# One level of a Strassen-type algorithm in the feed-forward products of a two-block network

## The chip, the cores and the metric

The kernel runs on one core of a Trainium2 chip. The metric is the device time of one launch in microseconds (us); lower is better. Inputs and output lie in the chip's memory (DRAM), and everything is float32.

## The reference, cut to what matters

Block 1 (gated linear attention with a pooling branch) and the attention of block 2 are the same before and after. The change concerns the feed-forward part at the end of block 2 (`x` has 1024 tokens by 1024 features, `D_FF` is 2816):

```python
def causal_dwconv(u, w, b):          # three taps over the tokens
    up = jnp.pad(u, ((0, 0), (CONV_WIDTH - 1, 0), (0, 0)))
    out = b + w[0] * up[:, 0:s_len]
    for kk in range(1, CONV_WIDTH):
        out = out + w[kk] * up[:, kk:kk + s_len]
    return out
...
    x = x + o @ w_out[l]
    h = rmsnorm_2(x, ffn_norm_g[l])
    u = causal_dwconv(h @ w_up[l], conv_w[l], conv_b[l])     # [1024, 5632]
    gate, val = jnp.split(u, 2, axis=-1)
    x = x + (jax.nn.silu(gate) * val) @ w_down[l]            # [1024, 2816] @ [2816, 1024]
return rmsnorm_2(x, final_norm_g)
```

## The kernel before

Everything is kept with features on the 128 partitions and the 1024 tokens along a row. A tile of x is 128 features by 1024 tokens, and there are 8 of them (`x2`). A product of two float32 matrices is made of three matmuls, since each operand is split into a high and a low part of a reduced format (`mm3`, L235 to L238): low times high, high times low, high times high. The splitting of weights (`load`, L225) is a cast on ScalarE (ACT) and a subtraction on GpSimd (POOL, L182); that of activations is on ACT and VectorE (DVE), or on POOL. One matmul takes 128 x 128 weights and 512 columns, half a row of tokens, into one of 8 PSUM banks.

The output projection of block 2 ends the attention part. Its loop over 8 column tiles `ct` scales a PSUM bank by a norm, adds it to `x1` (that is `x2[ct]`), squares the sum on ACT, and adds the squares up in `acc`, on POOL and for the last tile on DVE. The same loop makes the parts `u3h` and `u3l` of x for the up projection, without the norm: `R3`, one over the root mean square of each token, is put on afterwards, where the bank of the up product is read (`p_`, in `conv`). So the first up tile can begin while `acc` isn't complete (`gemm_late` with `k0=6`, which puts the norm's sum between the parts).

The feed-forward part has 22 tiles `k` of the hidden width; each has a gate tile `k` and a value tile `22 + k`. `up_group` makes two of them: for each, 48 matmuls for the gate tile, 48 for the value tile, the convolution (ACT scales by one tap, DVE adds the two others), the sigmoid on ACT, two products on DVE, and the split into `fh` and `fl` (POOL). `down` then takes the two tiles and adds their products with `w_dn`, 96 matmuls, to the 8 tiles of `x2`, bank by bank, on DVE. The up products of the next group are put ahead of the down products of this one, so that TensorE always has work. The last group's down products, the final norm and the result go by parts of the tokens (`SEQ`).

The order of the work on each engine is that of the program after a scheduler has merged the streams. All DMAs of this part are issued by SyncE (SP), in order. PSUM banks and the slots of SBUF (pool `sb`, 32 slots of a row; `wpool` with 2 raw and 4 split weight buffers) come free when their last reader is done.

Of the kernel before, what the change touches and what calls it, by code (L numbers as in the profile page):

```python
# [17 lines left out]
P = 128  # L18
# [40 lines left out]
# columns of the vector table (one value per partition and column)  # L59
# [11 lines left out]
# columns of the constant table  # L71
# [7 lines left out]
# the first column tile of each block of w_mod  # L79
# [16 lines left out]
def fused_blocks(ctx, tc, io, out, dbg=None):  # L96
# [11 lines left out]
    wpool = ctx.enter_context(tc.tile_pool(name="wpool", bufs=1))  # L108
    sb = ctx.enter_context(tc.tile_pool(name="sb", bufs=1))
# [8 lines left out]

    def ld(name):
# [10 lines left out]
    def ht(name, dt=F32):  # L130
        return sb.tile([P, HALF], dt, tag="h", bufs=NH, name=f"{name}_{uid()}")
# [16 lines left out]
    # ---- constants  # L148
# [31 lines left out]
    # ---- arithmetic helpers  # L180
# [6 lines left out]
    def split(src, hi, lo, eng=None, scale=None):  # L187
        """src (times scale, one value per partition) = hi + lo exactly, both in float32r."""
# [7 lines left out]
    def defer(ins, on):  # L196
        """Keeps an early-ready load from being issued before another step of the program."""
# [6 lines left out]
    def log_exp_table(after):  # L204
        """Loads the table that has both functions, past the last use of another."""
# [3 lines left out]
    def rstd(total, r, n, scale=1.0 / D):  # L209
        """r = 1 / sqrt(total * scale + eps): exp(-ln / 2), then one Newton step."""  # L210
# [9 lines left out]
    def sigmoid(src, o):  # L220
        """o = 1 / (1 + exp(-src)) as exp(-ln(1 + exp(-src)))."""
# [4 lines left out]
    # ---- products: weights are split into two float32r parts as they come in  # L226
# [8 lines left out]
    def mm3(ps, ah, al, bh, bl, first, last):  # L235
        nc.tensor.matmul(ps, ah, bl, start=first, stop=False)  # L236
        nc.tensor.matmul(ps, al, bh, start=False, stop=False)  # L237
        nc.tensor.matmul(ps, ah, bh, start=False, stop=last)  # L238
# [3 lines left out]
    def gemm(parts, xh, xl, ranges=XH, c=P, c0=0, m=P, per=4, ks=range(KD), tag="pp"):  # L242
        """A tile of output columns; gives a bank of PSUM for each range of tokens."""
# [24 lines left out]
    def bank_rstd(acc, r, scale=1.0 / D, tag="pp"):  # L268
        """r = 1 / sqrt(mean + eps) from sums over all partitions of acc [128, 1024]."""
# [7 lines left out]
    def need(key):  # L277
        """Emits fillers up to the one called key."""
# [3 lines left out]
    def weave(fill, chain):  # L282
        """Emits each filler (key, step, function) before the given step of the chain."""
# [23 lines left out]
    x1_d = [dtile(f"x1_d{k}") for k in range(KD)]  # L307
    ra_d = dtile("ra_d")
# [7 lines left out]
    # ================================================================== block 1  # L316
# [3 lines left out]
    # conditioning vectors through silu  # L320
# [1030 lines left out]
```

## Time and profile before

| what | us |
| --- | --- |
| median of 3 runs | 2675.21 (2672.87 to 2677.45) |
| span of the profiled execution | 2679.3 |
| TensorE (PE) busy in it | 2549.1 (95%) |
| DVE, ACT, POOL busy | 1505.9 (56%), 961.0 (36%), 809.5 (30%) |

The profiled execution is one launch of its own; its span stands beside the median of the timed runs. Matmuls overlap in the records, since one begins before the last has drained: the distance from one start to the next is what a matmul costs, not its duration. Times of a waiting operation are longer than those of a free one where it waits for a shared resource after it has begun. The page's 40 slices show PE at 9 of 10 almost everywhere from the second slice on. The rows themselves stand in a section further down.

### The profile page before, as it was taken

How to read it: one execution, taken by the hardware profiler on the slowest of the kernel's cores; microseconds unless marked ns; L12 is line 12 of the kernel's file. 1: busy time of each engine (PE TensorE's matmuls, PEld its weight loads, DVE VectorE, ACT ScalarE, POOL GpSimd, SP SyncE). 2: the span in 40 equal slices, each digit the busy share in tenths (PEclk: the TensorE clock that was granted, in tenths of full speed). 3: DMA queues.
4: the chain of work that ended last, by engine and by line, in shares of the span. 5: the costliest groups of instructions: out<-in, count | busy, mean ns of one | idle time of the engine just before them, and what ended most of it. 6: DMA issues, size and time to landing. Idle time of an engine off the chain costs nothing. (4 is left out here: it accounts for less than half of the span.)

```text
span 2679.3 us, 36279 instructions
## 1 busy us (share of the span) xinstructions
PE 2549.1 (95%) x14390; PEld 2015.2 (75%) x14390; DVE 1505.9 (56%) x2190; ACT 961.0 (36%) x1634; POOL 809.5 (30%) x592
## 2 busy tenths in 40 slices
PE   6989999999999999999999999999899999999996
PEld 3878977777787888876777766666688888888885
DVE  6363292765927223255766677788934444444456
ACT  4342262553734412332333443433422222222233
POOL 1432221221212224434233222233433333333334
PEclk9989999999999999999999999999999999999998
DMA  6423242433424553335444323430111111111112
GB/s 256 125 74 108 86 158 85 151 111 101 145 80 146 196 193 110 118 103 155 127 127 127 113 77 114 124 105 28 40 49 49 48 48 48 47 48 48 48 48 75
DMA packets 109113, 270.55 MB, mean 101 GB/s; under 512 B 13600, under 2 KB 18592, under 8 KB 108944
## 3 DMA queue, kind: packets, MB, share of 16 engines
q1 hardware_dynamic: 101648, 244.90, 28.3%
q0 software_dynamic: 7296, 23.34, 3.7%
q8 instruction: 113, 1.85, 0.3%
q14 instruction: 56, 0.46, 0.1%
HBM read 192.40 MB, written 71.57 MB: 99 GB/s over the span
## 5 line engine op out<-in xcount | busy, mean ns | idle before, releaser
L182 POOL TENSOR_TENSOR wlo<-wraw,whi 128x512 fp32r<-128x512 f32 (+1 forms) x363 | 537.3, 1482 | 1639.2 <-ACT whi L190 1593.1
L190 ACT CAST whi<-wraw 128x512 fp32r<-128x512 f32 (+1 forms) x363 | 223.8, 617 | 709.4 <-PE pp L238 617.6
L236 PE MATMUL pp<-hl,whi 128*128 128x512 f32 (+1 forms) x768 | 312.1, 407 | 4.8 <-DVE hl L185 4.8
L237 PE MATMUL pp<-hh,wlo 128*128 128x512 f32 (+1 forms) x768 | 307.2, 400 | 0.4 <-POOL wlo L182 0.4
L238 PE MATMUL pp<-hh,whi 128*128 128x512 f32 (+1 forms) x768 | 306.4, 399 | 0.0
L238 PE MATMUL pp<-u3h,whi 128*128 128x512 f32 x688 | 271.4, 395 | 0.0
L237 PE MATMUL pp<-u3h,wlo 128*128 128x512 f32 x688 | 271.0, 394 | 0.0
L236 PE MATMUL pp<-u3l,whi 128*128 128x512 f32 x688 | 270.2, 393 | 0.0
L182 DVE TENSOR_TENSOR x<-x,pp 128x512 f32<-128x512 f32 (+1 forms) x184 | 121.5, 664 | 208.5 <-PE pp L238 208.5
L236 PEld LDWEIGHTS pp<-hl,whi 128*128 128x128 f32 (+1 forms) x768 | 144.9, 189 | 42.5 <-DVE hl L185 5.8
L237 PEld LDWEIGHTS pp<-hh,wlo 128*128 128x128 f32 (+1 forms) x768 | 144.8, 189 | 38.9 <-issue 6.1
L238 PEld LDWEIGHTS pp<-hh,whi 128*128 128x128 f32 (+1 forms) x768 | 144.9, 189 | 33.7 <-issue 0.4
L1028 DVE COPY pt<-pg 128x512 f32<-128x512 f32 (+2 forms) x192 | 101.0, 553 | 92.5 <-PE pg L1026 91.8
L237 PEld LDWEIGHTS pp<-u3h,wlo 128*128 128x128 f32 x688 | 129.0, 188 | 30.9
L236 PEld LDWEIGHTS pp<-u3l,whi 128*128 128x128 f32 x688 | 129.2, 188 | 30.3
L238 PEld LDWEIGHTS pp<-u3h,whi 128*128 128x128 f32 x688 | 129.1, 188 | 30.1
L236 PE MATMUL pp<-fl,whi 128*128 128x512 f32 (+1 forms) x368 | 142.0, 386 | 0.0
L238 PE MATMUL pp<-fh,whi 128*128 128x512 f32 (+1 forms) x368 | 141.4, 384 | 0.0
L237 PE MATMUL pp<-fh,wlo 128*128 128x512 f32 (+1 forms) x368 | 140.8, 383 | 0.0
L185 DVE SCALAR_TENSOR_TENSOR t<-p,vec,t 128x1023 f32<-128x1023 f32 x88 | 122.1, 1395 | 33.1 <-ACT t L1144 32.1
L237 PE MATMUL pp<-uh,wlo 128*128 128x512 f32 x336 | 139.2, 414 | 0.0
L236 PE MATMUL pp<-ul,whi 128*128 128x512 f32 x336 | 138.3, 412 | 0.0
(384 smaller groups left out, 5434.0 us busy)
## 6 DMA issues: line engine op xcount, KB each, us to landing
wraw<-in_w_up SPq DMA_DIRECT2D x88, 256.0 KB
wraw<-in_w_qk SPq DMA_DIRECT2D x48, 256.0 KB
wm<-in_w_mod SPq DMA_DIRECT2D x24, 512.0 KB
wraw<-in_w_dn SPq DMA_DIRECT2D x44, 256.0 KB
x<-in_xT SPq DMA_DIRECT2D x16, 512.0 KB
wraw<-in_w_v SPq DMA_DIRECT2D x32, 256.0 KB
wraw<-in_w_out SPq DMA_DIRECT2D x32, 256.0 KB
q<-qs_d POOLq DMA_DIRECT2D x16, 512.0 KB, 5.0
```

The source lines that it names most:

```text
L182: return (eng or nc.vector).tensor_tensor(out=o, in0=a, in1=b, op=op)
L185: return (eng or nc.vector).scalar_tensor_tensor(out=o, in0=a, scalar=s, in1=b, op0=op0, op1=op1)
L190: nc.scalar.copy(hi, src)
L236: nc.tensor.matmul(ps, ah, bl, start=first, stop=False)
L237: nc.tensor.matmul(ps, al, bh, start=False, stop=False)
L238: nc.tensor.matmul(ps, ah, bh, start=False, stop=last)
L1028: nc.vector.tensor_copy(o, ps[:, :w])
```

## The change

Write the up product of one pair (gate tile `k` and value tile `22 + k`) as a 2 x 2 block product: the two tiles by two halves of the 1024 input features, times the two halves of the features by two halves of the tokens. Such a product needs 8 block products of 12 matmuls (4 tiles of 128 features, 3 matmuls each), or 7 with sums of blocks as operands (`seven` gives the weight side, `T` the x side). The change makes 7, in the order 1, 6, 2, 5, 7, 3, 4. Banks `al`, `be` and `ga` are added to by two or three products each, and read out in between. The down product is made the same way in four groups of 3, 3, 2 and 2 pairs of tiles (`DN_GROUPS`; tiles 20 and 21 are left to plain products at the end, as before). There each product's 4 banks take 12 matmuls from every pair of the group.

The operands must be split after they are summed, so the norm is put on x first (`normed`), and 28 parts of x are made ahead of the loop, every other lower part on POOL. All weights are summed by DVE as they come and split by ACT and POOL. The buffers don't hold both stages: x2 is written to DRAM (`x2_d`) and read again for the down stage, and each gated tile is written to `f_d` and read again. The pools are closed and opened anew at the start of the up products and of the down products; a pool `keep` of 8 rows stays (and the main pool of the earlier parts has 24 slots and not 32).

```diff
-NSLOT, NF, NT, NLD, NH, NQT = 32, 3, 2, 3, 5, 5
+NSLOT, NKEEP, NF, NT, NLD, NQT = 24, 8, 3, 2, 3, 5
+UP_RAW, UP_SUM, UP_W, UP_E = 6, 4, 5, 5
+DN_RAW, DN_SUM, DN_W = 34, 14, 3
+DN_GROUPS = [[(0, 3), (1, 4), (2, 5)], [(6, 9), (7, 10), (8, 11)], [(12, 14), (13, 15)], [(16, 18), (17, 19)]]
...
+        nc.sync.dma_start(x2_d[ct], x1)
...
-        u3h.append(b1k("u3h", F32R))
-        u3l.append(b1k("u3l", F32R))
-        split(x2[ct], u3h[ct], u3l[ct], None, V("ffg", ct))
-    R3 = b1k("R3")
-    u0, = gemm_late(
-        [[load(io["w_up"][0, j], 4, P) for j in range(2)]], u3h, u3l, tags=["lg"], k0=6, then=lambda: bank_rstd(acc, R3, tag="pg"),
-    )
...
+    for a, b in XH:
+        ps = get("pg")
+        nc.tensor.matmul(ps, ones, acc[:, a:b], start=True, stop=True)
+        total.append(ps)
+    front.close()
...
+    for ps in total:
+        R3.append(seg("R3", "R3", 2))
+        rstd(ps, R3[-1], HALF)
...
+    def xparts(src):
+        turn[0] += 1
+        return parts(src, "t", 28, nc.gpsimd if turn[0] % 2 else None)
...
+    for j in range(4):
+        T[1].append(xparts(normed(j, LOW)))
+    for j in range(4):
+        T[2].append(xparts(normed(j + 4, LOW)))
+    for j in range(4):
+        b12, b22 = normed(j, HIGH), normed(j + 4, HIGH)
+        b11, b21 = x2[j][:, LOW], x2[j + 4][:, LOW]
+        t3, t2 = seg("t3", "e", UP_E), seg("t2", "e", UP_E)
+        tt(t3, b22, b12, ALU.subtract)
+        tt(t2, t3, b11, ALU.add)
+        T[6].append(xparts(t2))
+        T[7].append(xparts(t3))
+        tt(b21, b21, t2, ALU.subtract)
+        tt(b12, b12, b11, ALU.subtract)
...
+    def seven(a11, a12, a21, a22, s1, s2):
+        yield 1, a11
+        tt(s1, a21, a22, ALU.add)
+        tt(s2, s1, a11, ALU.subtract)
+        yield 6, s2
+        yield 2, a12
+        yield 5, s1
+        tt(a11, a11, a21, ALU.subtract)
+        yield 7, a11
+        tt(s2, a12, s2, ALU.subtract)
+        yield 3, s2
+        yield 4, a22
...
+        for n, src in seven(*raw, s1, s2):
+            w = parts(src, "w", UP_W, nc.gpsimd)
+            wh, wl = (x.rearrange("p (k c) -> p k c", k=4) for x in w)
+            bank = {1: al, 2: al, 7: ga, 4: ga}.get(n, be)
+            for j in range(4):
+                th, tl = T[n][j]
+                mm3(bank, wh[:, j], wl[:, j], th, tl, j == 0 and n in (1, 6, 7), j == 3, True)
+            if n == 1:
+                p1 = seg("p1", "e", UP_E)
+                nc.scalar.copy(p1, al)
+            elif n == 2:
+                nc.scalar.copy(pg[:, LOW], al)
+            elif n == 6:
+                u = seg("u", "e", UP_E)
+                tt(u, p1, be, ALU.add)
...
+        tt(tg, tg, pg, ALU.mult)
+        tt(tg, tg, tv, ALU.mult)
+        nc.sync.dma_start(f_d[k], tg)
+    back.close()
...
+            for j in range(len(pairs)):
+                m, src = next(As[j])
+                wh, wl = parts(src, "w", DN_W, nc.gpsimd)
+                th, tl = parts(tsum(n, B[j], S[j]), "t", DN_W, nc.gpsimd if j else None)
+                for c in range(4):
+                    cs = slice(c * P, c * P + P)
+                    mm3(banks[c], wh[:, cs], wl[:, cs], th, tl, j == 0 and n in (1, 6, 7), j == len(pairs) - 1, True)
...
+                o = x2[o[0]][:, o[1]]
+                tt(o, o, banks[c], ALU.add)
+            if n == 1 and g == len(DN_GROUPS) - 1:
+                for c in range(4):
+                    for ct, half in ((c, HIGH), (c + 4, LOW), (c + 4, HIGH)):
+                        o = x2[ct][:, half]
+                        tt(o, o, p1[c], ALU.add, nc.gpsimd)
```

First place: POOL at the start of the up products. Before, after the last addition of squares (`acc`), it splits weights of the up products (`wlo`) and then the first gated tile (`fl`):

```order
L182 TENSOR_TENSOR wlo_16737<-wraw_16735,whi_16736 128x512
L182 TENSOR_TENSOR wlo_16743<-wraw_16741,whi_16742 128x512
L182 TENSOR_TENSOR wlo_16806<-wraw_16804,whi_16805 128x512
L182 TENSOR_TENSOR wlo_16812<-wraw_16810,whi_16811 128x512
L182 TENSOR_TENSOR fl_16730<-t_16646,fh_16729 128x1024
L182 TENSOR_TENSOR wlo_16883<-wraw_16881,whi_16882 128x512
L182 TENSOR_TENSOR wlo_16889<-wraw_16887,whi_16888 128x512
```

After, `lo` of `x_` and `t_` are operands of x (14 of them, the last ten shown), `lo_16770` ahead of these belongs to the weights of the first product, `lo_16790` to those of the second:

```order
L195 TENSOR_TENSOR lo_16649<-t_3061_16645,hi_16648 128x512
L195 TENSOR_TENSOR lo_16665<-t_3067_16661,hi_16664 128x512
L195 TENSOR_TENSOR lo_16681<-t_3073_16677,hi_16680 128x512
L195 TENSOR_TENSOR lo_16697<-t_3079_16693,hi_16696 128x512
L195 TENSOR_TENSOR lo_16707<-x_2764_15301,hi_16706 128x512
L195 TENSOR_TENSOR lo_16715<-x_2829_15573,hi_16714 128x512
L195 TENSOR_TENSOR lo_16723<-x_2886_15836,hi_16722 128x512
L195 TENSOR_TENSOR lo_16731<-x_2943_16099,hi_16730 128x512
L195 TENSOR_TENSOR lo_16739<-x_2886_15836,hi_16738 128x512
L195 TENSOR_TENSOR lo_16747<-x_2943_16099,hi_16746 128x512
L195 TENSOR_TENSOR lo_16790<-s_3113_16763,hi_16789 128x512
L195 TENSOR_TENSOR lo_16808<-wr_16756,hi_16807 128x512
```

The weights of the first pair's second product moved behind all the operands of x.

Second place: DVE in the middle of the up products. Before, the read-out of two banks (`p`), then the convolution's two steps (L185), the product with the sigmoid and that of gate and value:

```order
L182 TENSOR_TENSOR p_16879<-pp_16893,R_3051_16562 128x512
L182 TENSOR_TENSOR p_16879<-pp_16919,R_3051_16562 128x512
L185 SCALAR_TENSOR_TENSOR t_16880<-p_16879,vec,t_16880 128x1023
L185 SCALAR_TENSOR_TENSOR t_16880<-p_16879,vec,t_16880 128x1022
L182 TENSOR_TENSOR p_16948<-pp_16962,R_3051_16562 128x512
L182 TENSOR_TENSOR t_16880<-t_16880,sgf_17017 128x1024
L182 TENSOR_TENSOR p_16948<-pp_16988,R_3051_16562 128x512
L185 SCALAR_TENSOR_TENSOR t_16949<-p_16948,vec,t_16949 128x1023
L185 SCALAR_TENSOR_TENSOR t_16949<-p_16948,vec,t_16949 128x1022
L182 TENSOR_TENSOR t_16880<-t_16880,t_16949 128x1024
```

After, from the read-out of one pair's last but one bank to the `u` of the next (`s_` are sums of weights, L198 the convolution's steps, `pv` and `pg` the tiles that the banks go to):

```order
L195 TENSOR_TENSOR pg_17682<-p_3301_17703,pp_17685 128x512
L195 TENSOR_TENSOR s_3352_17986<-wr_17982,wr_17984 128x512
L195 TENSOR_TENSOR s_3353_17987<-s_3352_17986,wr_17978 128x512
L198 SCALAR_TENSOR_TENSOR t_17813<-pg_17682,vec,t_17813 128x1023
L195 TENSOR_TENSOR pv_17683<-u_17723,pp_17686 128x512
L198 SCALAR_TENSOR_TENSOR t_17813<-pg_17682,vec,t_17813 128x1022
L198 SCALAR_TENSOR_TENSOR t_17817<-pv_17683,vec,t_17817 128x1023
L195 TENSOR_TENSOR t_17813<-t_17813,pg_17682 128x1024
L198 SCALAR_TENSOR_TENSOR t_17817<-pv_17683,vec,t_17817 128x1022
L195 TENSOR_TENSOR u_17876<-p_3331_17856,pp_17838 128x512
```

The read-out `pv` of product 4 and that of the next pair's product 6 (`u`) now have convolution steps and a product ahead of them. On ACT the copy of the next pair's first bank (`p_`, L1240) stands behind the sigmoid (L1268) there:

```order
L1260 ACTIVATE t_17660<-pg_17529,vec 128x1024
L203 CAST hi_17761<-wr_17672 128x512
L1260 ACTIVATE t_17664<-pv_17530,vec 128x1024
L1268 ACTIVATE pg_17529<-t_17660 128x1024
L1240 COPY p_3301_17703<-pp_17684 128x512
L203 CAST hi_17779<-s_3293_17681 128x512
```

Third place: SP where the up products end. Before, the loads of weights go on in a row, of the up tiles and of the down tiles:

```order
L231 DMA wraw_21098<-in_w_up 128x512
L231 DMA wraw_21168<-in_w_dn 128x512
L231 DMA wraw_21206<-in_w_dn 128x512
L231 DMA wraw_21244<-in_w_dn 128x512
L231 DMA wraw_21282<-in_w_dn 128x512
L231 DMA wraw_21320<-in_w_dn 128x512
```

After, with `q_` the blocks of the first down group, from `f_d` and from the weights:

```order
L1273 DMA f_d_206<-t_19802 128x1024
L1273 DMA f_d_207<-t_19955 128x1024
L1291 DMA q_20129<-f_d_187 128x512
L1291 DMA q_20131<-f_d_190 128x512
L1291 DMA q_20133<-f_d_187 128x512
L1291 DMA q_20135<-f_d_190 128x512
L1291 DMA q_20137<-in_w_dn 128x512
L1291 DMA q_20139<-in_w_dn 128x512
L1291 DMA q_20141<-in_w_dn 128x512
L1291 DMA q_20143<-in_w_dn 128x512
L1291 DMA q_20145<-f_d_188 128x512
L1273 DMA f_d_208<-t_20108 128x1024
```

Loads of the first down group are issued ahead of the write of the last gated tile (`f_d_208`), and the rest of them, 15 loads and then the 8 of x2, behind it.

## Rows read from the trace of the kernel before

**Rows 1.** Page, part 1: busy time, share of the span, instructions, by engine.
```profile
PE 2549.1 (95%) x14390; PEld 2015.2 (75%) x14390; DVE 1505.9 (56%) x2190; ACT 961.0 (36%) x1634; POOL 809.5 (30%) x592
```

**Rows 2.** Windows: start:end, length, busy us (x instructions) by engine, granted clock, DMA.
```profile
1900.00:1950.00 50.00, 37.92 (x146) 28.51 (x145) 41.79 (x40) 20.52 (x24) 23.12 (x12) 0.90 0.12 37
...
2000.00:2050.00 50.00, 50.00 (x217) 40.55 (x217) 26.32 (x30) 11.72 (x14) 13.64 (x9) 1.00 0.16 48
...
2350.00:2400.00 50.00, 50.00 (x218) 40.50 (x217) 28.77 (x32) 14.63 (x17) 17.30 (x11) 1.00 0.17 48
...
2550.00:2600.00 50.00, 50.00 (x217) 40.52 (x216) 29.19 (x32) 14.63 (x17) 17.28 (x12) 1.00 0.16 47
```

**Rows 3.** Time line of TensorE, 1905 to 1931: start, us, operation, [idle before <-releaser].
```profile
1905.55 0.47 PE L236 MATMUL lg<-u3l,whi 128*128 128x512 f32 x1 [3.71 <-DVE t L182]
...
1907.04 0.63 PE L236 MATMUL lg<-u3l,whi 128*128 128x512 f32 x1
...
1907.46 0.63 PE L237 MATMUL lg<-u3h,wlo 128*128 128x512 f32 x1
...
1924.35 3.52 PE L272 MATMUL pg<-acc,ones 128*128 128x512 f32 x4 [7.67 <-DVE acc L182]
...
1930.47 0.39 PE L236 MATMUL pp<-u3l,whi 128*128 128x512 f32 x1
```

**Rows 4.** Time line of DVE, 1882 to 1931.
```profile
1882.08 1.28 DVE L182 TENSOR_TENSOR x<-x,t 128x512 f32<-128x512 f32 x2
...
1883.99 0.69 DVE L182 TENSOR_TENSOR x<-x,t 128x512 f32<-128x512 f32 x1
...
1886.73 2.90 DVE L182 TENSOR_TENSOR x<-x,t 128x512 f32<-128x512 f32 x1
...
1889.55 2.31 DVE L185 SCALAR_TENSOR_TENSOR u3l<-x,vec,u3h 128x1024 fp32r<-128x1024 f32 x1
...
1911.54 1.27 DVE L182 TENSOR_TENSOR t<-lg,rs 128x512 f32<-128x512 f32 x2
...
1930.57 0.68 DVE L185 SCALAR_TENSOR_TENSOR R<-rt,R 128x512 f32<-128x512 f32 x1
```

**Rows 5.** Time line of POOL, at the change-over and at 2039.
```profile
1886.52 2.56 POOL L182 TENSOR_TENSOR acc<-acc,sq 128x1024 f32<-128x1024 f32 x1 [4.40 <-ACT sq L1122]
...
1889.03 1.74 POOL L182 TENSOR_TENSOR wlo<-wraw,whi 128x512 fp32r<-128x512 f32 x1
...
1910.68 3.21 POOL L182 TENSOR_TENSOR acc<-acc,sq 128x1024 f32<-128x1024 f32 x1
...
2039.86 1.30 POOL L182 TENSOR_TENSOR wlo<-wraw,whi 128x512 fp32r<-128x512 f32 x1 [6.15 <-ACT whi L190]
```

**Rows 6.** Groups by line and form, 1940 to 2600: count, busy us, mean ns, idle before.
```profile
L182 POOL TENSOR_TENSOR wlo<-wraw,whi 128x512 fp32r<-128x512 f32 x120 | 164.0, 1367 | 392.8 <-ACT whi L190 392.6
...
L182 POOL TENSOR_TENSOR fl<-t,fh 128x1024 fp32r<-128x1024 f32 x21 | 51.1, 2433 | 60.8 <-ACT fh L190 60.8
...
L182 DVE TENSOR_TENSOR x<-x,pp 128x512 f32<-128x512 f32 x144 | 99.0, 688 | 194.9 <-PE pp L238 194.9
...
L185 DVE SCALAR_TENSOR_TENSOR t<-p,vec,t 128x1023 f32<-128x1023 f32 x41 | 58.6, 1429 | 30.8 <-ACT t L1144 30.8
...
L182 DVE TENSOR_TENSOR t<-t,sgf 128x1024 f32<-128x1024 f32 x21 | 25.7, 1225 | 4.4 <-ACT sgf L1166 4.1
...
L1166 ACT ACTIVATE sgf<-t 128x1024 f32<-128x1024 f32 x21 | 22.3, 1062 | 56.3 <-DVE t L185 56.3
```

**Rows 7.** Time lines of SP and ACT at the start: a load's issue, loads landing.
```profile
0.76 0.39 SPq L150 DMA_DIRECT2D vec<-in_vec  x1
...
2.95 0.21 ACT L322 ACTIVATE tsi<-vec 128x16 f32<-128x16 f32 x1 [0.92 <-DMA vec<-in_vec]
...
13.20 1.06 ACT L340 ACTIVATE sq<-x 128x1024 f32<-128x1024 f32 x1 [0.29 <-DMA x<-in_xT]
...
14.48 1.06 ACT L340 ACTIVATE sq<-x 128x1024 f32<-128x1024 f32 x1 [0.22 <-DMA x<-in_xT]
```

More of the change, by code (lines that the diff above doesn't have):

```diff
@@ L117, in b1k, with xk @@
         return bt(name, dt)[:, :L]
+    def xk(name, dt=F32):
+        return keep.tile([P, SLOT], dt, tag="x", bufs=NKEEP, name=f"{name}_{uid()}")[:, :L]
     def ld(name):
@@ L233, in load, with mm3 @@
         return hi.rearrange("p (k c) -> p k c", k=kh), lo_.rearrange("p (k c) -> p k c", k=kh)
[L235 to L238, printed above, removed]
+    def mm3(ps, ah, al, bh, bl, first, last, again=False):
+        nc.tensor.matmul(ps, ah, bl, start=first, stop=False, skip_group_check=again)
+        nc.tensor.matmul(ps, al, bh, start=False, stop=False, skip_group_check=again)
+        nc.tensor.matmul(ps, ah, bh, start=False, stop=last, skip_group_check=again)
     XH = [(0, HALF), (HALF, L)]
@@ L307, in fused_blocks @@
     x1_d = [dtile(f"x1_d{k}") for k in range(KD)]
+    x2_d = [dtile(f"x2_d{k}") for k in range(KD)]
+    f_d = [dtile(f"f_d{k}") for k in range(NFF)]
     ra_d = dtile("ra_d")
@@ L1110, in fused_blocks @@
     )
-    u3h, u3l = [], []
     acc = b1k("acc3")
@@ L1139, in conv @@
-    def conv(ct, banks=None):
-        p_, t = b1k("p"), b1k("t")
-        for ps, a, b in banks or gemm([load(io["w_up"][ct, j], 4, P) for j in range(2)], u3h, u3l):
-            tt(p_[:, a:b], ps, R3[:, a:b], ALU.mult)
+    total = []
+    for a, b in XH:
[3 more added lines that the diff above has]
+    front.close()
+    back = ExitStack()
+    sb = back.enter_context(tc.tile_pool(name="up", bufs=1, reuse_waits="tile"))
@@ new lines, in fused_blocks, with seg, parts @@
+    tags["h"] = ("e", UP_E)
+    def seg(name, tag, bufs, dt=F32):
+        return sb.tile([P, HALF], dt, tag=tag, bufs=bufs, name=f"{name}_{uid()}")
+    def parts(src, tag, bufs, eng):
+        hi, lo_ = seg("hi", tag + "h", bufs, F32R), seg("lo", tag + "l", bufs, F32R)
+        split(src, hi, lo_, eng)
+        return hi, lo_
+    R3 = []
+    for ps in total:
+        R3.append(seg("R3", "R3", 2))
+        rstd(ps, R3[-1], HALF)
+    es.close()
+    es = ExitStack()
+    get = psum_pool(es, pp=(HALF, 8))
@@ new lines, in fused_blocks, with normed @@
+    LOW, HIGH = slice(0, HALF), slice(HALF, L)
+    turn = [0]
+    def xparts(src):
+        turn[0] += 1
+        return parts(src, "t", 28, nc.gpsimd if turn[0] % 2 else None)
+    def normed(k, half):
+        x = x2[k][:, half]
+        stt(x, x, V("ffg", k), R3[0 if half is LOW else 1], ALU.mult, ALU.mult)
+        return x
+    T = {n: [] for n in range(1, 8)}
+    for j in range(4):
+        T[1].append(xparts(normed(j, LOW)))
+    for j in range(4):
+        T[2].append(xparts(normed(j + 4, LOW)))
@@ new lines, in fused_blocks @@
+    for j in range(4):
[9 more added lines that the diff above has]
+    for j in range(4):
+        T[5].append(xparts(x2[j][:, HIGH]))
+    for j in range(4):
+        T[3].append(xparts(x2[j + 4][:, HIGH]))
@@ L1144, in conv @@
+    def conv(ct, p_):
+        t = xk("t")
         nc.scalar.activation(t, p_, AF.Identity, scale=V("cw", 88 + ct), bias=V("cb", ct))
@@ L1176, in down @@
-    def down(grp, wd, c2, fh, fl, ranges=XH):
-        for cc in range(2):
-            ct = 2 * c2 + cc
-            for ps, a, b in gemm([wd], fh, fl, ranges, c0=cc * P, per=2, ks=range(2)):
-                tt(x2[ct][:, a:b], x2[ct][:, a:b], ps, ALU.add)
-    def load_down(grp, c2):
-        return load(io["w_dn"][grp, c2], 2, DV)
-    f = up_group(0)
-    for grp in range(NFF // 2 - 1):
-        nf = up_group(grp + 1)
-        for c2 in range(4):
-            down(grp, load_down(grp, c2), c2, *f)
-        f = nf
@@ L1193, in fused_blocks @@
-    wd = [load_down(NFF // 2 - 1, c2) for c2 in range(4)]
-    rF = b1k("rF")
+    for k in range(NFF):
+        pg, pv = up_pair(k)
+        tg, tv = conv(k, pg), conv(NFF + k, pv)
+        i = nc.scalar.activation(pg, tg, AF.Sigmoid)
+        if k == NFF - 1:
+            log_exp_table(i)
+        tt(tg, tg, pg, ALU.mult)
+        tt(tg, tg, tv, ALU.mult)
+        nc.sync.dma_start(f_d[k], tg)
+    back.close()
+    sb = ctx.enter_context(tc.tile_pool(name="down", bufs=1, reuse_waits="tile"))
@@ new lines, in fused_blocks, with in_half @@
+    fl_, wl_ = {}, {}
+    for k in (NFF - 2, NFF - 1):
+        for h, half in enumerate((LOW, HIGH)):
+            f = raw_tile("f")
+            nc.sync.dma_start(f, f_d[k][:, half])
+            fl_[k, h] = parts(f, f"f{k}{h}", 1, None)
+            w = raw_tile("wl")
+            nc.sync.dma_start(w, io["w_dn"][k, h])
+            wl_[k, h] = parts(w, f"v{k}{h}", 1, nc.gpsimd)
+    rF = [raw_tile("rF") for _ in range(2)]
+    def in_half(a, b):
+        return a // HALF, slice(a % HALF, a % HALF + b - a)
@@ L1196, in final, with last_down @@
+    def last_down(a, b):
+        h, ts = in_half(a, b)
+        for ct in range(KD):
+            cs = slice(ct % 4 * P, ct % 4 * P + P)
+            ps = get("pp")[:, : b - a]
+            for k in (NFF - 2, NFF - 1):
+                (wh, wl), (th, tl) = wl_[k, ct // 4], fl_[k, h]
+                mm3(ps, wh[:, cs], wl[:, cs], th[:, ts], tl[:, ts], k == NFF - 2, k == NFF - 1)
+            tt(x2[ct][:, a:b], x2[ct][:, a:b], ps, ALU.add)
     def final(a, b):
-        g = L // (b - a)
+        g = HALF // (b - a)
+        h, ts = in_half(a, b)
@@ L1226, in fused_blocks @@
         a, b = RNG[n]
+        h, ts = in_half(a, b)
         if what == "product":
-            for c2 in range(4):
-                down(NFF // 2 - 1, wd[c2], c2, *f, [(a, b)])
+            last_down(a, b)
         elif what == "squares":
```

146 lines of the change are left out of this document (102 added, 44 removed).

## The prediction

> **What bounds the kernel now.** I read the page's busy shares first, then the windows of the last 800 us, then the time lines around 1900 us. TensorE is busy 95% of the span [rows 1]. In the feed-forward part it is never idle: 50 us hold 217 or 218 matmuls, the granted clock is 1.00 (2.4 GHz), while DVE, ACT and POOL are busy 11 to 29 of 50 us and the DMA engines a sixth of the time [rows 2]. A 512-column matmul therefore costs 50/217.5 = 0.230 us, and each one that disappears there is worth 0.230 us as long as the others keep up. The one hole is the change-over from the output projection: the window from 1900 has 146 matmuls, 72 fewer (16.5 us). There TensorE waits for DVE's last addition of squares until 1924.35 and has finished the 48 matmuls of the first up tile at 1930.47 [rows 3].
>
> **What is removed.** Up: 22 x 2 tiles x 48 = 2112 matmuls become 22 x 7 products x 12 = 1848. Down: 20 of 22 tiles of the gated product, 960 matmuls, become 10 pairs x 7 x 12 = 840; the last two stay. That is 384 fewer, 384 x 0.230 = **88.4 us** less if TensorE stays as full as it was.
>
> **What two engines do to each other.** The price of everything added depends on one pattern of the change-over. A DVE addition of two SBUF tiles of 512 takes 0.69 us alone, 0.60 from one to the next (1882.08 and 1883.99 [rows 4]). At 1886.73 it takes 2.90 us: POOL has been in a 1024-wide addition since 1886.52 and ends at 1889.08 [rows 5]. POOL's next subtraction (1889.03) takes 1.74 us against 1.30 alone (2039.86 [rows 5]), and DVE's 1024-wide step at 1889.55 takes 2.31, against 1.2 for one of its size (1225 ns [rows 6]). So each waits until the other has nearly ended: POOL shuts DVE out for about 1.14 us with 512 elements and 2.28 with 1024, DVE shuts POOL out for about 0.60 and 1.20. A DVE operation that reads PSUM isn't touched: two at 1911.54 take 1.27 us in the midst of a POOL addition that runs from 1910.68 to 1913.89. The Trainium skill has this as a rule (GPSIMD Engine Reference, 1. Specifications): POOL's SBUF interfaces are shared with VectorE and contend with its operations that have two SBUF inputs. The rows of this trace agree; without the contention the sum would be that of the first rival.
>
> Before, in the feed-forward part, this costs nothing: POOL has 141 subtractions in 660 us [rows 6], some 7 per k of 33 us (144 matmuls). The change adds weight sums and operand sums on DVE, two SBUF inputs each, and raises POOL's subtractions to 7 in 19.3 us (84 x 0.230).
>
> **1. Start of the up products.** No product can begin before the norm R3 now, since x2 is normed first. The parts that DVE made for the old up products (u3l) go, which helps: DVE needs per column tile 4 x 0.60 plus one POOL addition of 2.28, 4.7 us; x of tile 1 is done at 1884.7 [rows 4], six tiles later it is 1912.9, and with the square and the last addition the sum of squares is there at about 1914 instead of 1924.35. From there to the low half of the norm 6.9 us pass, as before (1924.35 to 1931.25 [rows 3, 4]): 1920.9. Then DVE has 41 operations on SBUF pairs until the last of the operands t2 (norms, sums, every other lower part), 41 x 0.60 = 24.6, with 7 POOL subtractions between, 7 x 1.14 = 8.0. POOL's queue has all 14 lower parts of the operands ahead of the weights of the second product (the first of the orders above): 8 more subtractions against a busy DVE, 8 x 1.74 = 13.9. The second product starts at 1967.4, and about 2 us go to the clock, which after a hole of 3.71 us fell so that eight matmuls were 0.43 apart instead of 0.23 (1905.55 and 1907.04 [rows 3]). By then 12 matmuls are done; before, 48 were done at 1930.47. Loss: (1969.4 - 1930.5) + 36 x 0.230 = **47 us**. If the engines didn't shut each other out, DVE's 53 operations take 31.8 us, and the loss is 30; with a hop lost at some of the casts, 55.
>
> **2. The 22 pairs.** Per pair the shared side carries POOL 7 x 1.14 = 8.0 and DVE 4 weight sums x 0.60 and 6 operations of 1024 (4 convolution steps, 2 products) x 1.20 = 9.6, together 17.6 of 19.3 us: it fits, with little room. But a PSUM bank is now taken up again two products later, so TensorE waits for DVE and ACT inside a pair (the second order). From the end of product 4 of one pair to the start of product 5 of the next TensorE has 3 products, 8.3 us; in that time DVE's queue has the eviction pv (0.60), three convolution steps (3 x 1.20), one product with the sigmoid (1.20) and then the eviction u that product 5 waits for (0.69): 6.1 us alone [rows 6], 9.5 with three POOL subtractions between. ACT's copy p1, for which product 2 waits, stands behind the sigmoid, and that behind a convolution step. I take 1.0 us a pair, **22 us**; from 0 (DVE's 6.1 us fit) to 40 (DVE's 9.6 and five evictions of 0.69, and POOL's 8.0, all one after the other: 21.1 us a pair).
>
> **3. From up to down.** Before, the two stages were interleaved and there was no seam. Now the down loads take buffers of the closed pool, and SP has the write of the last gated tile in the midst of them (the third order). That write waits for the convolution of the last pair: after the last matmul an eviction, two steps, sigmoid, two products, some 7 us from [rows 6], 9 with POOL between. Behind it 12 loads of 256 KB must land until the third weight quarter of product 1 is there. 512 KB land every 1.28 us [rows 7], so the write and the 12 loads take 1.3 + 7.7 us at least, plus some 2.2 us from issue to landing (vec, 0.76 to 2.95 [rows 7]) and 1.3 + 0.6 for cast and subtraction. TensorE goes on 21 us after its last up matmul, and has done two products of 2.76 us in between: 15.5, with 2 us for the clock **18 us**; 12 if the write comes at 6 us, 28 if loads run at half that rate for a while.
>
> **4. Down.** A group of three pairs has 252 matmuls, 58.0 us. POOL: 21 weight and 14 operand parts, 35 x 1.31 = 45.9 us alone; DVE: 24 sums and 7 parts, 31 x 0.60 = 18.6. If each DVE operation delays POOL, POOL needs 64.5 us: 6.5 lost in each of two groups. A group of two has 38.6 us of TensorE; POOL 27.5 (32.7 in the third group, which also splits the last weights) and DVE 13.8: 2.7 and 8 lost. In the last group 12 additions of p1 to x2 stand in POOL's queue between two products (15.7 us), and TensorE has one product of 5.5 us and three buffers to cover them: some 10 of it are seen. All of it is 13 + 8 + 2.7 + 10 = 34, with half the delays 22: I take **27 us**, from 11 (the 12 additions alone) to 40 (and a late evicted bank in each product group).
>
> **5. At nothing.** The x2 writes (8) and gated-tile writes (22) are issued while the DMA engines are busy a sixth of the time; loads of weights wait behind them for well under a pair. The last two tiles and the final norm are as before; 3 us either way.
>
> **Sum.** -88.4 + 47 + 22 + 18 + 27 = **+26 us**. The profiled span is 2679.3, 4.1 above the median of 2675.2; the difference goes on the median: **2701 us**.
>
> **Rivals.** (a) *The shared side holds up*: POOL and DVE slip past each other, since POOL can run five buffers ahead in a pair. Then it is 30 + 0 + 15 + 11 = 56 us of losses, 2643 us, faster. For it: in the steady part of before POOL's mean is 1367 ns, only 70 above its best. Against it: that part had half the pairs of operands. The point is a loss of 88 us in all; with the start and the seam at 47 + 18 the pairs and the down groups must lose under 23. (b) *Gain and losses meet*: the start as worked, pairs at 0.3 us, down at its low end: 47 + 7 + 18 + 15 = 87, 2674 us. (c) *The pairs run at the pace of the shared side*, 21.1 us: 47 + 40 + 18 + 34 = 139, 2726 us. Speaking for it: DVE works in order, and an eviction behind a delayed step is late for the bank. (d) *Fewer matmuls than they cost*: 0.230 us could grow if TensorE's short holes (1 us a pair) draw the clock down; the hole of 3.71 us cost under 2 us of it [rows 3], so even one such fall in each pair is 22 x 1 to 1.6, some 22 to 35 us, 2730 us; the trace shows none after a short hole in its steady part, since that has none.
>
> **How the numbers follow.** The forecast and its neighbourhood (slower by 6 to 40 us) 0.42; (c) and (d) 0.21; (b), within 0.2% (5.4 us, about what a measurement of this kernel tells from no change), 0.10; (a) and what lies between it and (b) 0.27. Faster 0.27, same 0.10, slower 0.63. The low ends of all four losses give 53 (2640), the high ends 163 (2750); all at one end is unlikely: the range is 2648 to 2738. The likeliest sign alone has 2681 to 2738.
>
> **What the profile will show.** Right: 384 fewer matmuls; a hole of 40 us or more from about 1905 with 12 matmuls in it; POOL's 512 subtractions at a mean of over 1.5 us there; pairs of 20 to 21 us with holes before products 2 or 5, released by the p1 copy and the eviction u; a hole of 15 us at the seam, released by a DMA; another in the last group, with POOL in additions of p1. Wrong: pairs of 19.3 us, and POOL at 1.3 us next to a busy DVE; or a second product long before 1960.

## The result and the profile after

The changed kernel takes 2736.48 us, the median of 4 runs (2734.65 to 2742.16), against 2675.88 for the kernel before beside it: 1.023 times as long, with a 95% interval of 1.0215 to 1.0244. The forecast was 26 us slower; it is 60.6 us slower. The sign was right and the time lies within the range, but the size is more than twice the forecast.

The page of the changed kernel: part 1 (busy time, share of the span, instructions), and PE's busy tenths and the granted clock over 40 slices.

```profile
PE 2483.7 (91%) x14006; PEld 1951.1 (71%) x14006; DVE 1733.8 (63%) x2398; ACT 1064.3 (39%) x1850; POOL 1029.5 (38%) x734
...
PE   6989999999999999998999999997399999979876
...
PEclk9999999999999999999999999999599999989988
```

384 matmuls are gone (14390 in [rows 1], 14006 now), and TensorE is busy for 65 us less; but DVE is busy for 228 us more and POOL for 220 us more. The windows (columns as in [rows 2]) show where TensorE now stands still: at the start of the up products, a little everywhere in the pairs, at the seam between up and down, and in the last down group.

```profile
1900.00:1950.00 50.00, 13.26 (x31) 7.07 (x30) 45.52 (x53) 14.48 (x23) 18.87 (x11) 0.61 0.20 73
1950.00:2000.00 50.00, 28.98 (x112) 22.78 (x113) 34.63 (x36) 21.57 (x36) 33.17 (x21) 0.74 0.13 37
...
2150.00:2200.00 50.00, 47.86 (x207) 38.30 (x206) 34.23 (x36) 20.42 (x28) 28.01 (x18) 1.00 0.24 74
...
2400.00:2450.00 50.00, 36.83 (x145) 28.82 (x144) 31.99 (x33) 16.58 (x21) 15.24 (x11) 0.86 0.41 141
...
2600.00:2650.00 50.00, 39.69 (x172) 31.57 (x170) 41.61 (x50) 17.13 (x30) 38.64 (x29) 0.95 0.00 1
```

Where TensorE waited, over the up and down stages (view of waits: engine, operation, releaser, us in total, times, longest):

```profile
PE pp L250 <- ACT hi L203: 41.3, 4, 30.1
PE pp L251 <- POOL lo L195: 22.4, 4, 13.7
PE pp L250 <- DVE lo L195: 20.2, 10, 6.9
PE pp L250 <- ACT p L1240: 14.6, 20, 1.3
PE pp L250 <- DVE u L195: 12.8, 21, 0.7
```

The waits for `p` (the copy p1) and `u` are those named in the prediction, once or twice in every pair. The 30.1 us are the hole at the start, the 13.7 us the additions of p1 in the last group. The time lines of PE, of ACT and POOL, and of SP at these places:

```profile
1914.29 3.59 PE L1143 MATMUL pg<-acc,ones 128*128 128x512 f32 x4 [10.84 <-DVE acc L195]
...
1962.48 0.77 PE L250 MATMUL pp<-lo,hi 128*128 128x512 f32 x1 [30.09 <-ACT hi L203]
1970.16 0.80 PE L251 MATMUL pp<-hi,lo 128*128 128x512 f32 x1 [6.92 <-POOL lo L195]
...
2456.83 0.80 PE L251 MATMUL pp<-hi,lo 128*128 128x512 f32 x1 [1.45 <-POOL lo L195]
...
2656.36 0.80 PE L251 MATMUL pp<-hi,lo 128*128 128x512 f32 x1 [13.72 <-POOL lo L195]
```

```profile
1955.48 6.33 ACT L203 CAST hi<-x 128x512 fp32r<-128x512 f32 x12
1961.72 0.61 ACT L203 CAST hi<-s 128x512 fp32r<-128x512 f32 x1
...
1959.70 9.18 POOL L195 TENSOR_TENSOR lo<-x,hi 128x512 fp32r<-128x512 f32 x6
1968.85 1.26 POOL L195 TENSOR_TENSOR lo<-s,hi 128x512 fp32r<-128x512 f32 x1
...
2638.52 16.12 POOL L195 TENSOR_TENSOR x<-x,p 128x512 f32<-128x512 f32 x12
```

```profile
2431.24 0.36 SPq L1291 DMA_DIRECT2D q<-f_d  x1
2437.88 0.33 SPq L1273 DMA_DIRECT2D f_d<-t  x1
...
2445.94 2.31 SPq L1291 DMA_DIRECT2D q<-in_w_dn  x4
```

From the same time lines the whole difference of the spans, 2735.6 - 2679.3 = 56.3 us, can be added up. The spacing of matmuls from start to start was 0.2319 us in the steady part of before (2824 steps); after, between waits, 0.2275 in the pairs and 0.2272 in the down groups.

| part | working | us |
| --- | --- | --- |
| matmuls saved | 384 x 0.2319 | -89.0 |
| closer spacing of the others | some 2720 x 0.0045 | -12.2 |
| start | the second matmul of the second product at 1970.16 with 13 done, before 48 at 1930.47: 39.7 + 35 x 0.2319 | +47.8 |
| 22 pairs | 1970.16 to 2428.69 less 1835 x 0.2274 and 2.5 of low clock | +38.7 |
| seam, to the third down product | 2428.69 to 2456.83 less 25 x 0.2274 and 2.4 of low clock | +20.0 |
| rest of the down groups | 2456.83 to 2696.81 less 863 x 0.2272 and 10.2 of low clock | +33.7 |
| low clock (1.2 GHz) after holes | 2.5 + 2.4 + 10.2, matmuls 0.43 apart | +15.1 |
| last 256-column part and final norm | 38.8 against 36.7 | +2.1 |
| sum | | +56.2 |

### The profile page after: what moved, and what is told of

Read it like the earlier page. It is cut to its first block, busy times and chain, and to the rows that moved or that the text cites. A ratio compares the mean times of both kernels' runs of the same rounds, so it can differ in the third digit from the quotient of the medians.

```text
span 2735.6 us, 36557 instructions
## 1 busy us (share of the span) xinstructions
PE 2483.7 (91%) x14006; PEld 1951.1 (71%) x14006; DVE 1733.8 (63%) x2398; ACT 1064.3 (39%) x1850; POOL 1029.5 (38%) x734
## 5 line engine op out<-in xcount | busy, mean ns | idle before, releaser
L195 POOL TENSOR_TENSOR wlo<-wraw,whi 128x512 fp32r<-128x512 f32 (+2 forms) x231 | 351.5, 1525 | 1253.4 <-ACT whi L203 1217.2
L250 PE MATMUL pp<-lo,hi 128*128 128x512 f32 (+1 forms) x944 | 379.0, 402 | 98.1 <-ACT hi L203 41.3
L251 PE MATMUL pp<-hi,lo 128*128 128x512 f32 (+1 forms) x944 | 372.4, 394 | 22.4 <-POOL lo L195 22.4
L252 PE MATMUL pp<-hi,hi 128*128 128x512 f32 (+1 forms) x944 | 371.0, 393 | 0.0
L250 PEld LDWEIGHTS pp<-lo,hi 128*128 128x128 f32 x944 | 181.6, 192 | 161.2 <-issue 41.6
L203 ACT CAST whi<-wraw 128x512 fp32r<-128x512 f32 (+2 forms) x231 | 141.9, 615 | 332.0 <-PE pp L252 258.4
L251 PEld LDWEIGHTS pp<-hi,lo 128*128 128x128 f32 x944 | 181.9, 193 | 59.9 <-POOL lo L195 24.6
L252 PEld LDWEIGHTS pp<-hi,hi 128*128 128x128 f32 x944 | 181.8, 193 | 37.8
L195 POOL TENSOR_TENSOR lo<-wr,hi 128x512 fp32r<-128x512 f32 x88 | 163.0, 1852 | 72.5 <-ACT hi L203 62.5
L252 PE MATMUL pp<-uh,whi 128*128 128x512 f32 x336 | 135.3, 403 | 0.0
```

What stands on the lines that cost most here:

```text
L195: return (eng or nc.vector).tensor_tensor(out=o, in0=a, in1=b, op=op)
L203: nc.scalar.copy(hi, src)
L250: nc.tensor.matmul(ps, ah, bl, start=first, stop=False, skip_group_check=again)
L251: nc.tensor.matmul(ps, al, bh, start=False, stop=False, skip_group_check=again)
L252: nc.tensor.matmul(ps, ah, bh, start=False, stop=last, skip_group_check=again)
```

## The experiments

Two questions were open. Why does a pair take 20.9 us and not 19.1: because POOL and DVE shut each other out (theory P), or because of the order of DVE's and ACT's queues alone (rival O)? And how much of the start, the seam and the last group goes with what the prediction named?

**No lower parts by POOL in the pairs.**

```diff
-            w = parts(src, "w", UP_W, nc.gpsimd)
-            wh, wl = (x.rearrange("p (k c) -> p k c", k=4) for x in w)
+            w = seg("hi", "wh", UP_W, F32R)
+            nc.scalar.copy(w, src)
+            wh = wl = w.rearrange("p (k c) -> p k c", k=4)
```

> Changed kernel, but in the 22 up pairs POOL makes no lower part of the weights: the high part stands in its place in the products, so the result lacks the lower parts; matmuls, DVE and ACT are as before. Theory P (the waits inside a pair, 27.4 us before products 2 and 5, come from POOL and DVE shutting each other out): without POOL's 7 subtractions a pair the two waits sum to under 8 us, a pair takes 19.3 to 19.7 us in place of 20.6 to 21.6, the time falls by 25 to 35 us to about 2705. Rival O (DVE's and ACT's own queue order, an eviction behind the convolution, is late anyway): waits stay above 18 us, the time falls by less than 10.

Measured: 2691.23 us (2690.47 to 2693.28), 45 us less than the changed kernel. From 1990 on the view of waits lists none in the pairs, and a window there holds as many matmuls as fit (columns as before):

```profile
2150.00:2200.00 50.00, 50.00 (x223) 41.26 (x221) 33.65 (x39) 23.53 (x32) 0.00 (x0) 1.00 0.23 74
```

A pair takes 19.06 us (mean of 21), in place of 20.91. In a pair DVE and ACT had the same operations in the same order as in the changed kernel, so the order alone doesn't make the waits: rival O falls, theory P holds. The gain is 10 us above what was expected, since nothing at all of the waits is left in the pairs (some 39 us); the other 6 us lie outside the pairs.

Groups by form show which steps were held up: the convolution's steps in front of the two evictions, first in the changed kernel (2000 to 2400), then in this run (2000 to 2380).

```profile
L198 DVE SCALAR_TENSOR_TENSOR t<-pg,vec,t 128x1023 f32<-128x1023 f32 x19 | 31.8, 1673 | 0.0
L198 DVE SCALAR_TENSOR_TENSOR t<-pg,vec,t 128x1022 f32<-128x1022 f32 x19 | 29.5, 1555 | 0.0
L198 DVE SCALAR_TENSOR_TENSOR t<-pv,vec,t 128x1022 f32<-128x1022 f32 x19 | 44.1, 2319 | 0.0
L195 DVE TENSOR_TENSOR u<-p,pp 128x512 f32<-128x512 f32 x19 | 12.8, 675 | 0.0
...
L198 DVE SCALAR_TENSOR_TENSOR t<-pg,vec,t 128x1023 f32<-128x1023 f32 x20 | 25.6, 1281 | 1.9 <-ACT t L1261 1.8
L198 DVE SCALAR_TENSOR_TENSOR t<-pg,vec,t 128x1022 f32<-128x1022 f32 x20 | 25.5, 1277 | 0.0
L198 DVE SCALAR_TENSOR_TENSOR t<-pv,vec,t 128x1022 f32<-128x1022 f32 x20 | 25.5, 1277 | 0.0
```

With POOL at work the two steps of the gate tile, which the sigmoid and behind it the copy p1 wait for, take 0.67 us longer together, and the last step before `u` 1.04 us (in all 19 pairs a POOL subtraction had begun 0.10 to 0.24 us ahead of it). The eviction `u` itself, which reads PSUM, takes 0.68 us although POOL is in a subtraction all the while in each of the 19 pairs. A wait of TensorE for p1 is 0.73 us in the mean and one for `u` 0.61. DVE also waits for POOL to have read sums of weights, but behind `u`, where it has room: it then still stands idle for a product of TensorE (view of waits of the changed kernel, DVE, 2000 to 2400).

```profile
DVE pg L195 <- PE pp L252: 38.2, 19, 2.0
```

**The convolution behind the next pair's evictions.** Nothing is changed but the order on DVE and ACT: the sigmoid behind the next pair's copy p1, the value tile's first step and the product behind its `u`, the second step and the last product behind its `v` (`on` is that eviction, `defer` keeps an instruction behind it).

```diff
+        i = nc.scalar.activation(pg, tg, AF.Sigmoid)
+        defer(i, on)
...
+        on = yield 6
+        steps(NFF + k, pv, tv, on, (1,))
+        defer(tt(tg, tg, pg, ALU.mult), on)
+        on = yield 5
+        steps(NFF + k, pv, tv, on, (2,))
+        defer(tt(tg, tg, tv, ALU.mult), on)
```

> Changed kernel with the same operations, but the order on two queues set by hand: the sigmoid of a pair behind the next pair's first copy p1 on ACT, and the value tile's convolution and the two products behind the next pair's evictions u and v on DVE. Rival O: the waits before products 2 and 5 go (from 27.4 us to under 6), the time falls by 30 to 40 us to about 2700. Theory P alone (17.6 us of shared side in 19.1 us of matmuls): the waits move to the evictions v and pv and at most 12 us are won.

Measured: 2727.98 us (2722.52 to 2734.51), 8.5 us less. The waits moved, as theory P alone had it (view of waits, the pairs of this kernel):

```profile
PE pp L250 <- DVE pv L195: 24.6, 19, 1.3
PE pp L250 <- DVE v L195: 1.3, 1, 1.3
```

A pair takes 20.62 us in place of 20.91. Another order makes another eviction late, and wins 0.3 us a pair.

**The operands of x in the order of the products.** So that the first pair's weights stand between them in POOL's queue: `operands(n)` makes `T[n]` when the first pair comes to product n.

```diff
         for n, src in seven(*raw, s1, s2):
             w = parts(src, "w", UP_W, nc.gpsimd)
+            operands(n)
```

> Changed kernel, the x operands of each product made when the first pair comes to that product, four fewer kept sums, so that POOL's queue has the first pair's weights between the operands and not behind all 14. If the hole at the start is POOL's queue (the step of the prediction): the second product begins at about 1945 in place of 1970, the first pair ends near 1968 in place of 1989, 18 to 25 us less: about 2714. If it is DVE's number of operations: the hole is cut in pieces, each product waits for its operands, and under 8 us are won.

Measured: 2738.12 us (2736.16 to 2744.11), no better. The second product does begin early, at 1941.46 (expected: 1945); but each later product waits for its own operands, and the second pair then for the parts of its weights and for `u`: from the last addition of squares to the second pair's start it is 67.5 us in place of 76.6, and the second pair then takes 32.2 us in place of 20.6. So the order of the queues sets when the second product begins, but not when the first two pairs are done: the work for the operands has to be done either way. The rival holds.

**The seam and the last group.**

```diff
-        nc.sync.dma_start(f_d[k], tg)
+        if k < NFF - 1:
+            nc.sync.dma_start(f_d[k], tg)
...
+        if g == 0:
+            nc.sync.dma_start(f_d[NFF - 1], tg)
...
-            if n == 1 and g == len(DN_GROUPS) - 1:
-                for c in range(4):
-                    for ct, half in ((c, HIGH), (c + 4, LOW), (c + 4, HIGH)):
-                        o = x2[ct][:, half]
-                        tt(o, o, p1[c], ALU.add, nc.gpsimd)
+            if g == len(DN_GROUPS) - 1 and n != 4:
+                for ct, half, c in adds[:2]:
+                    o = x2[ct][:, half]
+                    tt(o, o, p1[c], ALU.add)
+                del adds[:2]
```

> Changed kernel with two edits at places far apart: the write of the last gated tile behind the first down group's 24 loads, and the 12 additions of p1 on DVE, two behind each product of the last group, in place of 12 in a row on POOL. If the write holds the loads up: the third of the first three down products starts at about 2450 in place of 2456.8, and the hole between is 5 to 7 us shorter; if the loads' own time does: under 2. The hole of 13.7 us in the last group goes; if POOL's row of 12 is its cause 10 to 14 us are won there, if the shared side is full anyway (DVE 35 and POOL 21 operations on pairs, some 45 us for 38 of matmuls) 4 to 7. Sum: 2717 to 2725.

Measured: 2725.3 us (2721.74 to 2732.23), 11 us less. SP now goes on from 2429.40 without a pause, and from the last up matmul to the third down product it is 21.3 us in place of 25.9: 4.6 won, a little under the 5 to 7. That is the upper end, since other kernels here with the write in its old place have 24.0 to 25.0. The last group takes 46.6 us in place of 54.6: 8.0 won, between the two cases, since a hole is left there that a lower part on DVE ends:

```profile
2640.92 0.79 PE L250 MATMUL pp<-lo,hi 128*128 128x512 f32 x1 [5.83 <-DVE lo L195]
```

**All lower parts on DVE.** If a POOL subtraction costs DVE 1.14 us of waiting and DVE does it in 0.60, the cheapest place for it is DVE, although DVE is the busier engine.

```diff
-        return parts(src, "t", 28, nc.gpsimd if turn[0] % 2 else None)
+        return parts(src, "t", 28, None)
...
-            w = parts(src, "w", UP_W, nc.gpsimd)
+            w = parts(src, "w", UP_W, None)
...
-                wh, wl = parts(src, "w", DN_W, nc.gpsimd)
-                th, tl = parts(tsum(n, B[j], S[j]), "t", DN_W, nc.gpsimd if j else None)
+                wh, wl = parts(src, "w", DN_W, None)
+                th, tl = parts(tsum(n, B[j], S[j]), "t", DN_W, None)
```

> Changed kernel with all lower parts of the up and down stages (operands and weights) made on DVE and none on POOL, except those of the last two plain tiles; nothing is left out. Theory P in its strict form (a POOL subtraction holds DVE up for about 1.14 us while DVE does it in 0.60): a pair is then DVE's own 16.8 us, below the 19.1 of its matmuls, so pairs take 19.1 to 19.5 (from 20.9), a down group of three pairs DVE's 56.4 against 57.3 of matmuls, 58 to 61 (from 69.3), the start some 8 us less: about 2736 - 33 - 25 - 8 = 2670. Rival L (DVE, at 17 of 19 us, is late with each lower part, since it stands behind evictions and steps in one queue): pairs at 20.5 or more, the down groups as before, 2725 or more.

Measured: 2669.03 us (2660.8 to 2672.49, 10 runs), 0.9972 of before (0.9962 to 0.9982): 67 us less than the changed kernel, by this edit alone. A pair takes 19.25 us, the second down group 57.1 in place of 69.3, and the way from the squares to the second pair 67.2 in place of 76.6. POOL is idle in these windows and DVE is busy 44 and 49 of 50 us, and TensorE has no hole:

```profile
2150.00:2200.00 50.00, 50.00 (x221) 41.15 (x220) 44.43 (x56) 23.53 (x32) 0.00 (x0) 1.00 0.26 74
2450.00:2500.00 50.00, 50.00 (x222) 41.40 (x222) 49.34 (x82) 20.68 (x37) 0.00 (x0) 1.00 0.39 112
```

The Trainium skill says (GPSIMD Engine Reference, 4.1 Engine selection) that element-wise work belongs on VectorE, POOL being some two times slower with two inputs; the trace agrees (1.30 against 0.69), and the runs show that here the slower engine costs the faster one its time too.

**The same with the seam and the additions.** Both edits together.

> As the run with all lower parts on DVE, with the late write of the last gated tile and the additions of p1 spread over the last group on DVE as well. Theory P: seam 4 us and last group 6 to 8 us less than that run, about 2659, faster than the kernel before by half a per cent. Rival L: the added 12 operations of DVE take back what is won in the last group, and the seam alone is left (4 us).

Measured: 2658.03 us (2655.75 to 2659.57), 0.9937 of before (0.9922 to 0.9952). 18.7 us from the last up matmul to the third down product; the last two groups together 93.3 us in place of 99.3. Theory P's 2659 is met.

**A part of it left on POOL.** As the last, with

```diff
+    return parts(src, "t", 28, nc.gpsimd if turn[0] % 4 == 3 else None)
...
+            w = parts(src, "w", UP_W, nc.gpsimd if n in (1, 2, 4) else None)
...
+                wh, wl = parts(src, "w", DN_W, nc.gpsimd if j == 0 else None)
```

> As the run before in this list, but POOL keeps 3 of 7 weight parts of a pair, 7 of 28 operands and one of five or of three lower parts of a down product. Strict P (each POOL subtraction costs DVE 1.14 and spares it 0.60): a pair needs 16.8 + 3 x 0.54 = 18.4 us, still under 19.1, but with less room: pairs 0 to 0.5 us longer than with all on DVE, down groups 2 to 4 longer; 0 to 15 us slower than that run. If POOL's work partly lies beside DVE's evictions from PSUM (which it doesn't hold up), it is 2 to 10 us faster than that run.

Measured: 2692.25 us (2689.76 to 2696.17), 34 us slower than with all on DVE, more than either case. A pair takes 20.67 us again, with three subtractions on POOL. The time lines of POOL, DVE and PE in one pair show why the sum alone is too kind (with DVE's four lower parts and five evictions it is 9.6 + 4 x 0.60 + 3 x 1.14 + 5 x 0.69 = 18.9 us, below the 19.1 of the matmuls):

```profile
2150.54 1.46 POOL L195 TENSOR_TENSOR lo<-wr,hi 128x512 fp32r<-128x512 f32 x1 [9.94 <-ACT hi L203]
```

```profile
2150.77 2.31 DVE L198 SCALAR_TENSOR_TENSOR t<-pv,vec,t 128x1022 f32<-128x1022 f32 x1
2153.00 0.68 DVE L195 TENSOR_TENSOR u<-p,pp 128x512 f32<-128x512 f32 x1
```

```profile
2153.73 0.50 PE L250 MATMUL pp<-lo,hi 128*128 128x512 f32 x1 [1.54 <-DVE u L195]
```

One POOL subtraction begins 0.23 us ahead of the last convolution step before `u`; the step takes 2.31 us in place of the 1.27 that it takes alone, `u` is late by as much, and TensorE waits 1.54 us. Of the three it is this one that counts, and it comes at the same place in each pair. It does matter where in the chain the two meet, not only how often.

**Lower parts of one pair on POOL in the last group only.** As the second last, with `nc.gpsimd if g == 3 and j == 0 else None` for the weights of the down products.

> As the run with all lower parts on DVE, the late write and the spread additions, but in the last down group POOL splits the weights of the group's first pair (7 of 28 lower parts). That group took 52.9 us there, DVE's own sum being 56 operations on pairs and 28 evictions at 0.60, 50.4 us, and 45.3 with 7 on POOL in the mixed run. Strict P counts each moved part at 1.14 - 0.60 = 0.54 us more on the shared side, so 52.9 + 3.8 = 57; if POOL's parts lie beside the 28 evictions from PSUM, 45 to 47, and the time 6 to 8 us less, about 2651.

Measured: 2657.2 us (2655.33 to 2660.63), no different. The group still takes 53.0 us; the last two groups together take 94.6 us in place of 93.3. Neither case was right. The same code of the last group took 45.3 us in the mixed run, behind a third group of 45.5; here the third group takes 41.6. So DVE seems to come into the last group with arrears, and its time in that group alone isn't the thing to compare; that reading wasn't tested.

**Operands in turn, with POOL out of the way.** The last kernel with the edit of the third run.

> As the run before in this list, with the x operands made in the order of the first pair's products. With POOL out of the way DVE's work for the operands (about 64 operations, 39 us) still precedes the end of the first pair; if DVE's amount bounds the start, the first pair ends 5 to 9 us earlier and later pairs keep 19.3 us: about 2644; if DVE's arrears are carried into the next pairs, as in the run that changed this order alone, it is within 3 us of the run before.

Measured: 2654.12 us (2653.49 to 2659.48, 5 runs), 0.9929 of before (0.9915 to 0.9942): the lowest median, though its runs overlap with those of the last two kernels. From the squares to the second pair it is 62.7 us in place of 67.2, but the second pair takes 21.9 in place of 19.3; 3 us less in the median, at the edge of what the second case allows, and not all of it from the start: the last two down groups, whose code is the same, take 91.0 in place of 94.6. DVE's arrears are carried on, as in the third run. The page of this kernel:

```profile
PE 2470.2 (93%) x14006; PEld 1948.6 (73%) x14006; DVE 1782.4 (67%) x2687; ACT 1064.2 (40%) x1850; POOL 585.7 (22%) x449
```

**The layout of the moving operand.** The closer spacing of the matmuls, with the 28 operands of x as pairs in rows of 1040 elements (as every tile of the kernel before is), and in rows of 1024.

```diff
+            if turn[0] % 2:
+                wide[d] = sb.tile([P, SLOT], F32R, tag=d, bufs=14, name=f"{d}_{uid()}")
+            o = HALF if turn[0] % 2 == 0 else 0
+            res.append(wide[d][:, o : o + HALF])
```

> Changed kernel, the x operands of the up products laid as two halves of rows of 1040 elements, as in the kernel before, and not as tiles of 512. It tests the matmul's spacing, 0.2319 us in the steady part of before and 0.2275 between waits in the up stage after. If the layout of the moving operand sets it: 0.231 to 0.232 in the up stage, 8 us more. If not: 0.2275 as it was, and the time within 5 us.

> Changed kernel with the x operands as halves of rows of 1024 elements (rows of 1040 gave a spacing of 0.2307 us against 0.2275 with tiles of 512). If the row's length of 1040 sets the spacing: 0.2275 in the up stage. If the sharing of one row by two operands does: 0.2307.

Measured: the mean distance of two matmuls between waits in the up stage is 0.2307 us with rows of 1040 and 0.2275 with rows of 1024 (and 0.2275 with tiles of 512). The single times, 2729.46 and 2732.03 us, say nothing of so small a difference. So the row length of 1040 (with the start addresses that it gives) accounts for 0.0032 of the 0.0044 us; where the rest comes from is open.

## Why the prediction was right in sign and wrong in size

- **The gain.** 88.4 was forecast and 89.0 came, and 12.2 more that the prediction didn't have, from the closer spacing. The rows before could not show it: every x operand there lies in rows of 1040.
- **The start, 47 us.** 47.8, and 2.5 of low clock, of which the 47 held 2. The squares were there at 1914.2 (forecast 1914; in part luck, since in the other kernels the same code took until some time between 1908.6 and 1916.8), the low half of the norm at 1921.6 (1920.9), and the second product could go on at 1970.2 (1967.4). What it said of the cause was only half so. The first matmul of that product needs no lower part of its weights, and it too had to wait until 1962.48, for ACT, whose cast of these weights stands behind the casts of all the operands. Without lower parts of the weights on POOL it began no earlier: 47.4 us after the first matmul of the squares' sum in the first run and 47.7 with all on DVE, against 48.2. POOL's queue cost the 7.7 us from 1962.48 to 1970.16, and the third run shows that another order moves the wait into the next pairs.
- **The pairs, 22 us taken, 0 to 40 allowed.** 38.7: here the prediction failed, at the step that takes 1.0 us a pair; it was 1.76. The places were right (products 2 and 5, p1 and u) and the cause was right (the first run); the size wasn't, for two reasons. The waits are 27.4 us in the view, not 22; and each costs TensorE some 0.27 us more than the idle time that the trace gives, which counts from the modelled end of the matmul before (0.39 us after its start, not 0.2275), and the first matmul after a wait is followed 0.34 us later: 41 waits, 11 us, a term that the prediction didn't have. The prediction weighed the shared side at 17.6 of 19.3 us and took this fit for room. But DVE works in order: it stands waiting at a step of two SBUF inputs, 2.32 us in place of 1.28 just before u, and the eviction behind it cannot go. The serial bound that it put at the end of its range as unlikely, DVE's 9.6 and 3.4 and POOL's 8.0, 21.1 us a pair, lies close to the 20.91 measured; that the sum sets the pace isn't shown, and the closeness may be luck. DVE was busy for 289 of the 400 us from 2000 on and waited for TensorE for 38 of them, and the run with three subtractions on POOL took 20.67 with a sum of 18.9.
- **The seam, 18 us.** 20.0 and 2.4 of low clock, of which the 18 held 2. Late by the write of the last tile, as said (SP's pause from 2431.6 to 2437.88); moving the write won at most 4.6 us of it.
- **Down, 27 us.** 33.7, within the bounds of 11 to 40; the 12 additions cost 13.7 in place of 10. But 10.2 of low clock after the holes of these groups come on top, 43.9 together. The forecast put the clock at nothing here, and this second step misses by as much as the pairs, 17 us each; the closer spacing took 12 of the two back.
- **The clock.** Two falls of 2 us each were counted, in the start and the seam; from the second product on there are eight, at the start, in the seam and after the longer holes of the down groups, 15.1 us together. The forecast put more falls into a rival of the pairs, and there none came: with holes of up to 1.3 us the granted clock of these windows is 1.00.
- **The rivals.** (d), 2730 us, lies nearest by the number, but through falls of the clock in the pairs, which did not come. (c), the pairs at 21.1 us, 2726 us, came nearest in what the pairs did. With the serial bound for the pairs (18 us more) and the clock after every long hole (11 more) the same sum would have been 2730.

## What to carry to other kernels

Where VectorE and GpSimd both work on pairs of SBUF operands, add their times up as if they were one engine, VectorE's evictions included, before counting on the overlap; if the sum reaches TensorE's, take work off GpSimd even if VectorE is the busier one. A sum that fits isn't enough: look for a GpSimd operation that begins just ahead of a VectorE step with an eviction behind it (one of these in each pair cost 1.5 us). A change that saves TensorE work is worth its matmuls only as long as nothing becomes late in the new, shorter time; and a wait costs more than its idle time in the trace. Moving one late step forward in a queue may only make the next one late: it won 0.3 us a pair in the changed kernel, and nothing at its start.

## What the runs showed of the hardware

A 1022-wide step of VectorE with two SBUF inputs takes 1.28 us with GpSimd idle and 2.32 us (mean of 19) just behind the start of a GpSimd subtraction of 512; an eviction with one PSUM input takes 0.68 us (mean of 19) in the midst of one.

Two matmuls of 512 columns follow each other in 0.2275 us when the moving operand lies in rows of 512 or 1024 elements of 4 bytes, and in 0.2307 us in rows of 1040, at a granted clock of 1.00 in both; the kernel before, with all operands in rows of 1040, has 0.2319. Over the 3120 such matmuls of its feed-forward part 0.0032 us each are 10 us.
